# Loading the border rows and the first tile of a pooling mixer in single loads, with another order of its loads and steps

## The chip, the cores and the metric

The program runs on one core of a Trainium2 chip. The metric is the device time of one execution in microseconds; the lower, the better. A core has engines that run side by side, each through its own list of instructions in order: TensorE (PE) does matrix products, VectorE (DVE), ScalarE (ACT) and GpSimd (POOL) work on tiles, SyncE (SP) issues loads and stores. They wait for each other through semaphores.

## The reference, cut to what matters

A trunk of two layers on 512 tokens of width 1024, in float32. Layer 0 mixes tokens by pooling, layer 1 by stick-breaking attention; each mixer is followed by an MLP with a squared ReLU, and every block is wrapped in RMS norms. The change lies in the pooling mixer of layer 0, which is the first thing that the program does:

```
def pool_mixer(h, w_grp, scale):            # h: (1, 512, 1024)
    cp = cumsum of h along the tokens, with a zero in front
    for g, w in enumerate((2, 4, 8, 16)):   # four groups of 256 channels
        window sum over the last w tokens / min(pos + 1, w) - h
    y = einsum('bsgc,gcd->bsgd', y, w_grp)  # 256 x 256 per group
    return y * scale

x = x + rms_norm(pool_mixer(rms_norm(x, mix_pre_g[0]), pool_w[0], pool_scale[0]), mix_post_g[0])
h = rms_norm(x, mlp_pre_g[0])
x = x + rms_norm(square(relu(h @ w_up[0])) @ w_down[0], mlp_post_g[0])
...                                          # layer 1: attention, then its MLP
```

## The kernel before, in words

The 512 tokens lie in four tiles x0 to x3 of 128 tokens each, with the channels along the free axis. Pooling is a matrix product: for each group of channels a banded matrix of 128 x 128 (`bands`) holds the window's weights less the identity. The band is scaled row by row with the token's reciprocal norm and multiplied on TensorE with the tile. The first 15 tokens of tiles 1 to 3 need rows of the tile before, so the 30 rows around each of the three borders are held apart in a fourth operand, `edge` (90 rows), which has a band of its own with 46 columns.

The mixer is written as steps, each a letter with a tile (0 to 3; 4 is `edge`) and mostly a half h of the channels. The list `MIX_ORDER` names the steps one after another, and every engine runs its own steps in that order; nothing else sorts them. The letters that matter here:

- `z n`: n products of a constant bf16 tile into a bank that nobody reads (`busy`, function at L652 to L654): it only keeps TensorE at work.
- `S h`, `C h`: the channel scale, one row in memory, is spread over 128 partitions by a product with ones (PE, L658) and copied to `scale` (ACT, L661).
- `L i b`: a 256-column piece of the group weights `pw` is multiplied by the norm's gain (`gc`) and by `scale` (DVE, L667).
- `q t`, `r t`, `b t`: sum of squares of a tile (ACT, L679), its power -0.5 (POOL, L690), the scaled band (DVE, L698).
- `P t h`, `c t h`: the pooling product (PE, L708) and its copy to `yt` (ACT, L723; three pieces for `edge`, L719).
- `M t h`, `s t h`, `g t h`: the group product of `yt` with `pw` (PE, L731), its sum of squares (ACT, through L250), its product with the gain row (DVE, L739).
- `e`, `E`, `A`: norm and residual; `w`, `v`, `N`: the next norm; `T`, `H`, `X`: transposes (PE, L765) and the split of the result into a high and a low float32r part (ACT L773, DVE L777).
- `h j`, `l j`, `U j`: the same split for the first four blocks of the MLP's up weights (ACT L785, DVE L789) and their product with the first 256 tokens (PE, L607 to L609). `U0` is the first product of the MLP.

All loads before are issued by SP, in the order in which they are written. A load's tile is not waited for by SP itself; but the program has eight semaphores for loads in turn, so that SP issues a load only after the load eight places earlier has landed.

From `U0` on the program is a long stream of products: the MLP of layer 0 (its down product in Strassen-Winograd form, L497), the projections and attention, the second MLP. The table that the change replaces ends with `U0` to `U3`.

Of the kernel before, what the change touches and what calls it, by code (L numbers as in the profile page):

```python
# [15 lines left out]
P = 128  # L16
D = 1024
S = 512
# [13 lines left out]
TS = [slice(t * P, (t + 1) * P) for t in range(T)]  # L32
NS = [slice(0, 512), slice(512, 1024)]
# [7 lines left out]

MIX_ORDER = [
    (w[0], [int(c) for c in w[1:]])
    for w in """z8 q0 S0 r0 C0 b0 S1 z1 P00 L01 C1 L02 L00 P01 L03 L12 c00 c01 M00 q4 L10 r4 L11 s00 L13 b4 q1 r1 M01 s01
    e0 P40 b1 P11 P10 q2 c40 r2 c11 E0 q3 g00 b2 g01 r3 c10 P21 A0 b3 M11 w0 M10 s11 c21 v0 P31 N00 g11 s10
    T00 P30 h0 M21 e1 c31 g10 E1 c30 N01 A1 P20 H00 T01 w1 X00 h1 v1 l0 s21 N11 M30 T11 c20 N10 T10 H01 M20
    l1 H11 X11 H10 X10 s30 M31 X01 h2 s20 h3 g21 l2 s31 g20 e2 g30 E2 e3 E3 U0 A2 w2 g31 U1 A3 v2 U2 l3 N20
    w3 T20 H20 v3 N31 T31 N30 N21 T30 H31 X20 X31 T21 H30 X30 U3 H21 X21""".split()
]


# [10 lines left out]
EDGE, REST, BORDER = 30, 114, 46  # L62
# [7 lines left out]
def trunk(ctx, tc, x, consts, gcol, grow, pw, wup, wdn, wq, wk, wv, wo, out):  # L70
    nc = tc.nc
# [4 lines left out]
    psum = pool("psum", 8, space=bass.MemoryType.PSUM)  # L76
    dram = pool("dram", space=bass.MemoryType.DRAM)

    nc.scalar.preload_act_table_set("sigmoid_and_others")

    uid = [0]

    def name(s):
# [7 lines left out]
    xt = [keep.tile([P, D + 2], F32, tag=f"x{t}", name=f"x{t}") for t in range(T)]  # L91
    ident = keep.tile([P, P], F32, tag="ident", name="ident")
    gc = keep.tile([P, 3 * KC + 32], F32, tag="gc", name="gc")[:, : 3 * KC]
    for n in NS:
        nc.sync.dma_start(xt[0][:, n], x[TS[0], n])
    mhalf = keep.tile([P, 1], F32, tag="mhalf", name="mhalf")
    nc.vector.memset(mhalf, -0.5)

# [123 lines left out]
    for l in range(2):  # L222
        if l == 1:
            n = len(queue)
# [387 lines left out]
    with tc.tile_pool(name="mix0", bufs=1, reuse_waits="tile") as mp:  # L612
# [7 lines left out]
        edge = mp.tile([3 * EDGE, D + 2], F32, tag="edge", name="edge")  # L620
# [4 lines left out]
        BANDS = (P, REST, BORDER)  # L625
        starts = [0, 4 * P, 4 * (P + REST)]
        bands = mp.tile([P, 4 * sum(BANDS)], F32, tag="bands", name="bands")
        wpool = [mp.tile([P, D], F32, tag=f"pw{i}", name=f"pw{i}") for i in range(2)]
        nc.sync.dma_start(bands[:, : 4 * P], consts[:, P : 5 * P])
        nc.sync.dma_start(row[:1], grow[R_SCALE : R_SCALE + 1, :])  # L630
        nc.sync.dma_start(gc, gcol)
        for i in range(2):
            nc.sync.dma_start(wpool[i], pw[i])
        for i in range(3):
            lo = (i + 1) * P - EDGE // 2
            nc.sync.dma_start(edge[i * EDGE : (i + 1) * EDGE, :D], x[lo : lo + EDGE, :])
        nc.sync.dma_start(xt[1][:, :D], x[TS[1], :])
        nc.sync.dma_start(bands[:, 4 * P :], consts[:, 5 * P :])
        nc.sync.dma_start(xt[2][:, :D], x[TS[2], :])
        gpost = gain_row(R_MIX_POST0)  # L640
        nc.sync.dma_start(xt[3][:, :D], x[TS[3], :])
# [171 lines left out]
    with tc.tile_pool(name="att", bufs=1, reuse_waits="tile") as ap:  # L813
# [79 lines left out]
        for lo, n in SEG.values():  # L893
            c = min(n - P, 1)
            d = begin[:, lo + n - P - c : lo + n]
# [178 lines left out]
```

## Time and profile before

| | |
|---|---|
| time, median of 3 runs | 963.49 us (961.94 to 963.75) |
| profiled execution: its time, its span | 967.47 us, 965.7 us |
| busy share of the span: PE, PEld, DVE, ACT, POOL | 98%, 83%, 74%, 59%, 15% |
| mean granted TensorE clock | 0.991 |
| instructions | 12404 |
| moved by the DMA engines | 157.03 MB, 163 GB/s on average |

The span runs from the first instruction to the last; the 1.77 us between it and the execution's own time lie around it. PE is TensorE's products, PEld its loads of the stationary operand, which overlap them. The granted clock is the share of TensorE's full rate that the chip let it have. In a table of stretches each row gives, for one stretch of time, the busy microseconds of every engine with the number of instructions in brackets, then the granted clock, the mean busy share of the 16 DMA engines and what they moved in GB/s.

### The profile page before, as it was taken

What the parts mean: (1) busy time and instruction counts of PE and PEld (TensorE: products, weight loads), DVE (VectorE), ACT (ScalarE), POOL (GpSimd) and SP (SyncE); (2) the same over time, 40 slices, a digit from 0 to 9 for tenths busy, and PEclk for the clock granted to TensorE, in tenths of its full rate; (3) what the DMA queues carried; (4) which work ended last, traced back from release to release, by engine and by line L of the source; (5) the groups of instructions that cost most, each with busy time, mean ns of one, the idle gap of its engine ahead of it and who ended that gap; (6) DMA issues with size and microseconds to landing.
All of it is one profiled execution on the core that took longest, in us unless ns stands there. A gap on an engine that the chain in (4) does not pass through costs nothing.

```text
span 965.7 us, 12404 instructions
## 1 busy us (share of the span) xinstructions
PE 947.1 (98%) x4761; PEld 806.2 (83%) x4761; DVE 711.1 (74%) x736; ACT 566.9 (59%) x974; POOL 142.1 (15%) x108
## 2 busy tenths in 40 slices
PE   8999999999999999999999999989999999999997
PEld 6998888888788888899799997888888888888885
DVE  3865798997988966576477787855596776957956
ACT  5667889697684747456666562546445454443632
POOL 1210310402203114000000000302040300303003
PEclk8999999999999999999999999999999999999999
DMA  7343979688596850521534233231513233132012
GB/s 261 135 173 123 354 234 356 259 283 327 199 354 249 311 194 1 200 98 53 219 130 174 88 139 124 108 133 66 190 50 131 109 106 135 44 131 109 27 40 87
DMA packets 43683, 157.03 MB, mean 163 GB/s; under 512 B 4494, under 2 KB 4878, under 8 KB 43625
## 3 DMA queue, kind: packets, MB, share of 16 engines
q1 hardware_dynamic: 43625, 156.25, 45.4%
q8 instruction: 37, 0.61, 0.2%
q14 instruction: 21, 0.17, 0.1%
HBM read 122.68 MB, written 33.55 MB: 162 GB/s over the span
## 4 chain that ended last, share of the span: by engine, by line
PE 73%; DVE 11%; DMA 5%; issue 5%; ACT 5%; POOL 0%; POOLq 0%; DVEq 0%; SPq 0%; ACTq 0%
PE ps L497 18%; PE ps L608 11%; PE ps L607 11%; PE ps L609 11%; PE ps L268 4%; PE ps L269 4%; PE ps L267 4%; DMA xn<-in_wdn 3%; DVE w L247 2%; DMA raw<-in_wup 2%; PE ps L957 2%; PE ps L947 2%; DVE w L134 2%; DVE e L471 2%; PE ps L731 1%
## 5 line engine op out<-in xcount | busy, mean ns | idle before, releaser
L497 PE MATMUL ps<-w,a 128*128 128x512 f32 x1176 | 278.2, 390 | 1.2 <-DVE a L247 1.2
L608 PE MATMUL ps<-xnl,w 128*128 128x512 f32 (+1 forms) x712 | 262.8, 369 | 0.1
L609 PE MATMUL ps<-xnh,w 128*128 128x512 f32 (+1 forms) x712 | 262.5, 369 | 0.0
L607 PE MATMUL ps<-xnh,w 128*128 128x512 f32 (+1 forms) x712 | 262.4, 370 | 0.0
L497 PEld LDWEIGHTS ps<-w,a 128*128 128x128 f32 x1176 | 220.6, 188 | 48.0 <-DVE a L247 2.4
L609 PEld LDWEIGHTS ps<-xnh,w 128*128 128x128 f32 x712 | 135.0, 190 | 22.2
L608 PEld LDWEIGHTS ps<-xnl,w 128*128 128x128 f32 x712 | 135.0, 190 | 22.0 <-DVE xnl L247 0.3
L607 PEld LDWEIGHTS ps<-xnh,w 128*128 128x128 f32 x712 | 134.7, 190 | 21.8
L134 DVE TENSOR_TENSOR w<-raw,w 128x1024 fp32r<-128x1024 f32 x62 | 82.3, 1327 | 65.3 <-ACT w L132 65.2
L132 ACT CAST w<-raw 128x1024 fp32r<-128x1024 f32 x62 | 64.9, 1049 | 81.4 <-PE ps L609 76.2
L506 DVE TENSOR_TENSOR y<-ps,y 128x512 f32<-128x512 f32 x124 | 83.1, 683 | 33.2 <-PE ps L497 33.1
L246 ACT CAST a<-r 128x768 fp32r<-128x768 f32 (+1 forms) x60 | 47.6, 793 | 63.3 <-PE ps L497 39.2
L452 POOL TENSOR_TENSOR s<-r 128x768 f32<-128x768 f32 (+1 forms) x10 | 21.4, 2144 | 371.3 <-ACT r L530 352.7
L246 ACT CAST w<-e 128x1536 fp32r<-128x1536 f32 (+1 forms) x30 | 42.0, 1399 | 53.8 <-DVE e L471 42.6
L247 DVE TENSOR_TENSOR a<-r,a 128x768 fp32r<-128x768 f32 (+1 forms) x60 | 60.0, 1002 | 16.5 <-ACT a L246 16.4
L292 POOL TENSOR_TENSOR y<-y,grow 128x512 f32<-128x512 f32 x12 | 18.7, 1562 | 314.2 <-ACT xn L250 314.2
L247 DVE TENSOR_TENSOR w<-e,w 128x1536 fp32r<-128x1536 f32 (+1 forms) x30 | 59.6, 1988 | 3.1 <-ACT w L246 2.7
L452 POOL TENSOR_TENSOR r<-r 128x768 f32<-128x768 f32 (+1 forms) x20 | 50.5, 2523 | 66.1 <-DVE a L247 65.3
L929 DVE TENSOR_TENSOR_SCAN e<-u,begin 128x1280 f32<-128x1280 f32 x16 | 45.1, 2822 | 13.3 <-ACT u L923 13.0
L143 ACT ACTIVATE apart<-apart,gc 128x128 f32<-128x128 f32 (+1 forms) x132 | 43.0, 407 | 0.0
L250 ACT ACTIVATE xn<-y 128x512 f32<-128x512 f32 (+1 forms) x25 | 15.4, 616 | 41.6 <-DVE y L359 41.5
L529 ACT ACTIVATE r<-ps 128x512 f32<-128x512 f32 x56 | 33.0, 590 | 6.8 <-PE ps L609 6.8
(137 smaller groups left out, 1492.5 us busy)
## 6 DMA issues: line engine op xcount, KB each, us to landing
raw<-in_wup SPq DMA_DIRECT2D x62, 512.0 KB, 3.9
w<-kept SPq DMA_DIRECT2D x58, 512.0 KB, 4.2
kept<-wx SPq DMA_DIRECT2D x30, 512.0 KB, 5.0
w<-in_wdn SPq DMA_DIRECT2D x8, 1536.0 KB, 6.7
kept<-apart SPq DMA_DIRECT2D x24, 512.0 KB, 4.3
xn<-in_wdn SPq DMA_DIRECT2D x8, 1536.0 KB, 9.2
raw<-in_wdn SPq DMA_DIRECT2D x8, 512.0 KB, 3.7
apart<-in_wk SPq DMA_DIRECT2D x7, 512.0 KB, 6.4
```

The lines of the kernel that those rows point to most:

```text
L132: nc.scalar.copy(hi, raw)
L134: nc.vector.tensor_tensor(out=lo, in0=raw, in1=hi.bitcast(F32), op=ALU.subtract)
L143: nc.scalar.mul(c, c, gc[:, lo + k : lo + k + 1])
L246: latest["act"] = nc.scalar.copy(hi, src)
L247: latest["dve"] = nc.vector.tensor_tensor(out=lo, in0=src, in1=hi.bitcast(F32), op=ALU.subtract)
L452: sub = lambda out, x, y, op=ALU.subtract: nc.gpsimd.tensor_tensor(out=out, in0=x, in1=y, op=op)
L497: nc.tensor.matmul(bank, a[:, x, q, TS[t]], w[:, z, q], start=start and q == 0 and k == 0, stop=q == self.n - 1 and k == 2, skip_group_che ...
L506: nc.vector.tensor_tensor(out=part, in0=bank, in1=part, op=ALU.add)
L607: nc.tensor.matmul(pu[:, cols], wh[:, k, :], xnh[:, k, cols], start=k == 0, stop=False)
L608: nc.tensor.matmul(pu[:, cols], wh[:, k, :], xnl[:, k, cols], start=False, stop=False)
L609: nc.tensor.matmul(pu[:, cols], wl[:, k, :], xnh[:, k, cols], start=False, stop=k == KC - 1)
L929: nc.vector.tensor_tensor_scan(out=e[:, ::-1], data0=u[:, 1:][:, ::-1], data1=begin[:, ::-1], initial=0.0, op0=ALU.mult, op1=ALU.max,)
```

## The change

1. The first tile x0 comes in one load of 128 x 1024 instead of two of 128 x 512.
2. The norm columns `gc` are issued by ACT's queue, ahead of its table load, instead of by SP.
3. The three loads of border rows become one: a view of x with three dimensions (3 borders, 30 rows, 1024 channels) is written to the 90 rows of `edge`.
4. The order of the loads: `pw0` now stands ahead of the scale row, and the second part of `bands` ahead of x1.
5. `MIX_ORDER` is another list. It holds the same steps and two `z2` more, that is four more constant products.

```diff
 MIX_ORDER = [
     ...
-    for w in """z8 q0 S0 r0 C0 b0 S1 z1 P00 L01 C1 L02 L00 P01 L03 L12 c00 c01 M00 q4 L10 r4 L11 s00 L13 b4 q1 r1 M01 s01
-    e0 P40 b1 P11 P10 q2 c40 r2 c11 E0 q3 g00 b2 g01 r3 c10 P21 A0 b3 M11 w0 M10 s11 c21 v0 P31 N00 g11 s10
+    for w in """z8 S0 q0 r0 C0 S1 C1 b0 L03 z1 P00 c00 L00 P01 c01 q4 L02 L01 r4 L13 L11 L10 M00 L12 b4 s00 q1 M01 s01 r1
+    q2 b1 e0 r2 g01 z2 P40 c40 z2 P10 P11 c10 M10 c11 M11 g00 E0 q3 A0 w0 r3 b2 v0 b3 s10 N00 g10 P20 P30 s11 P31
...
-    nc.scalar.preload_act_table_set("sigmoid_and_others")
...
-    for n in NS:
-        nc.sync.dma_start(xt[0][:, n], x[TS[0], n])
+    nc.sync.dma_start(xt[0][:, :D], x[TS[0], :])
+    nc.scalar.dma_start(gc, gcol)
+    nc.scalar.preload_act_table_set("sigmoid_and_others")
...
-        nc.sync.dma_start(bands[:, : 4 * P], consts[:, P : 5 * P])
+        nc.sync.dma_start(wpool[0], pw[0])
         nc.sync.dma_start(row[:1], grow[R_SCALE : R_SCALE + 1, :])
-        nc.sync.dma_start(gc, gcol)
-        for i in range(2):
-            nc.sync.dma_start(wpool[i], pw[i])
-        for i in range(3):
-            lo = (i + 1) * P - EDGE // 2
-            nc.sync.dma_start(edge[i * EDGE : (i + 1) * EDGE, :D], x[lo : lo + EDGE, :])
+        nc.sync.dma_start(wpool[1], pw[1])
+        around = x[P - EDGE // 2 : S - EDGE // 2, :].rearrange("(i r) d -> i r d", r=P)[:, :EDGE]
+        nc.sync.dma_start(edge[:, :D], around)
+        nc.sync.dma_start(bands[:, 4 * P :], consts[:, 5 * P :])
         nc.sync.dma_start(xt[1][:, :D], x[TS[1], :])
-        nc.sync.dma_start(bands[:, 4 * P :], consts[:, 5 * P :])
         nc.sync.dma_start(xt[2][:, :D], x[TS[2], :])
```

(The load of the first part of `bands` is still issued, right behind x0.)

Two places show how the order moves. The first is SP's list of loads from the program's start. Before (`x_70` is x0, `x_71` x1, `x_72` x2; `pw_99` and `pw_100` are the two halves of the group weights):

```order
L95 DMA x_70<-in_x 128x512 x2
L629 DMA bands<-in_consts 128x512
L630 DMA row<-in_grow 1x1024
L631 DMA gc<-in_gcol 128x24
L633 DMA pw_99<-in_pw 128x1024
L633 DMA pw_100<-in_pw 128x1024
L636 DMA edge<-in_x 30x1024 x3
L637 DMA x_71<-in_x 128x1024
L638 DMA bands<-in_consts 128x640
L639 DMA x_72<-in_x 128x1024
```

Before, the scale row was the fourth load and stood ahead of 1 MB of `pw`.

After (`x_69`, `x_70`, `x_71` are x0, x1, x2; `pw_100` and `pw_101` the two halves):

```order
L92 DMA x_69<-in_x 128x1024
L627 DMA bands<-in_consts 128x512
L629 DMA pw_100<-in_pw 128x1024
L630 DMA row<-in_grow 1x1024
L631 DMA pw_101<-in_pw 128x1024
L633 DMA edge<-in_x 90x1x1024
L634 DMA bands<-in_consts 128x640
L635 DMA x_70<-in_x 128x1024
L636 DMA x_71<-in_x 128x1024
```

The scale row moved behind the first half of `pw`, `edge` became one load, and x1 moved behind the rest of `bands`.

The second place is TensorE between the pooling of tile 0 and that of tile 2, around the product with `edge`. Before:

```order
L708 MATMUL ps_152<-band_138,x_70 128x128 x4
L731 MATMUL ps_161<-pw_99,yt 128x256 x4
L731 MATMUL ps_178<-pw_100,yt 128x256 x4
L708 MATMUL ps_185<-band_173,edge 128x46 x8
L708 MATMUL ps_196<-band_194,x_71 128x114 x4
L708 MATMUL ps_201<-band_194,x_71 128x114 x4
L708 MATMUL ps_223<-band_218,x_72 128x114 x4
L731 MATMUL ps_231<-pw_100,yt 128x256 x4
L731 MATMUL ps_237<-pw_99,yt 128x256 x4
```

Here the product with `edge` is followed by three pooling products (two of x1, one of x2) and then by the two group products of tile 1.

After, from the two group products of tile 0 on:

```order
L728 MATMUL ps_163<-pw_100,yt 128x256 x4
L728 MATMUL ps_174<-pw_101,yt 128x256 x4
L651 LDWEIGHTS warm
L651 MATMUL ps_118<-warm 128x512
L651 LDWEIGHTS warm
L651 MATMUL ps_118<-warm 128x512
L705 MATMUL ps_191<-band_169,edge 128x46 x8
L651 LDWEIGHTS warm
L651 MATMUL ps_118<-warm 128x512
L651 LDWEIGHTS warm
L651 MATMUL ps_118<-warm 128x512
L705 MATMUL ps_205<-band_183,x_70 128x114 x4
```

Two constant products now stand ahead of the product with `edge` and two behind it. Behind these rows come the second pooling product of x1 and the group products of tile 1, and only then those of x2 and x3. From `U0` on every engine's list is the same as before.

More of the change, by code (lines that the diff above doesn't have):

```diff
@@ L43 @@
     (w[0], [int(c) for c in w[1:]])
-    for w in """z8 q0 S0 r0 C0 b0 S1 z1 P00 L01 C1 L02 L00 P01 L03 L12 c00 c01 M00 q4 L10 r4 L11 s00 L13 b4 q1 r1 M01 s01
-    e0 P40 b1 P11 P10 q2 c40 r2 c11 E0 q3 g00 b2 g01 r3 c10 P21 A0 b3 M11 w0 M10 s11 c21 v0 P31 N00 g11 s10
-    T00 P30 h0 M21 e1 c31 g10 E1 c30 N01 A1 P20 H00 T01 w1 X00 h1 v1 l0 s21 N11 M30 T11 c20 N10 T10 H01 M20
-    l1 H11 X11 H10 X10 s30 M31 X01 h2 s20 h3 g21 l2 s31 g20 e2 g30 E2 e3 E3 U0 A2 w2 g31 U1 A3 v2 U2 l3 N20
-    w3 T20 H20 v3 N31 T31 N30 N21 T30 H31 X20 X31 T21 H30 X30 U3 H21 X21""".split()
+    for w in """z8 S0 q0 r0 C0 S1 C1 b0 L03 z1 P00 c00 L00 P01 c01 q4 L02 L01 r4 L13 L11 L10 M00 L12 b4 s00 q1 M01 s01 r1
+    q2 b1 e0 r2 g01 z2 P40 c40 z2 P10 P11 c10 M10 c11 M11 g00 E0 q3 A0 w0 r3 b2 v0 b3 s10 N00 g10 P20 P30 s11 P31
+    h0 e1 E1 c20 g11 A1 N01 c30 c31 P21 T00 H00 w1 h1 l0 M20 v1 X00 c21 s20 M30 T01 N11 T11 s30 N10 T10 H11
+    l1 H10 g30 X11 H01 M21 M31 s21 h2 s31 X10 X01 g21 U0 g20 e2 E2 l2 e3 U1 g31 A2 E3 h3 w2 v2 A3 l3 U2 N21
+    w3 v3 N20 T20 N30 T30 H20 H30 N31 X20 T21 T31 H31 X30 U3 H21 X31 X21""".split()
 ]
@@ L627, in trunk @@
         bands = mp.tile([P, 4 * sum(BANDS)], F32, tag="bands", name="bands")
+        nc.sync.dma_start(bands[:, : 4 * P], consts[:, P : 5 * P])
         wpool = [mp.tile([P, D], F32, tag=f"pw{i}", name=f"pw{i}") for i in range(2)]
-        nc.sync.dma_start(bands[:, : 4 * P], consts[:, P : 5 * P])
+        nc.sync.dma_start(wpool[0], pw[0])
         nc.sync.dma_start(row[:1], grow[R_SCALE : R_SCALE + 1, :])
-        nc.sync.dma_start(gc, gcol)
-        for i in range(2):
-            nc.sync.dma_start(wpool[i], pw[i])
-        for i in range(3):
-            lo = (i + 1) * P - EDGE // 2
-            nc.sync.dma_start(edge[i * EDGE : (i + 1) * EDGE, :D], x[lo : lo + EDGE, :])
+        nc.sync.dma_start(wpool[1], pw[1])
+        around = x[P - EDGE // 2 : S - EDGE // 2, :].rearrange("(i r) d -> i r d", r=P)[:, :EDGE]
+        nc.sync.dma_start(edge[:, :D], around)
+        nc.sync.dma_start(bands[:, 4 * P :], consts[:, 5 * P :])
         nc.sync.dma_start(xt[1][:, :D], x[TS[1], :])
-        nc.sync.dma_start(bands[:, 4 * P :], consts[:, 5 * P :])
         nc.sync.dma_start(xt[2][:, :D], x[TS[2], :])
```

## The prediction

> **What bounds the kernel now.** I read the table of stretches first, then TensorE's instructions in order of time, then the waits behind the mixer. TensorE up to `U0`:
>
> ```profile
> 1.31 3.59 PE L654 MATMUL ps<-warm 128*128 128x512 bf16 x8 [1.31 <-POOL warm L615]
> 4.82 3.08 PE L658 MATMUL ps<-row,ones 128*128 128x512 f32 x4
> 7.73 0.38 PE L654 MATMUL ps<-warm 128*128 128x512 bf16 x1
> 7.95 1.95 PE L708 MATMUL ps<-band,x 128*128 128x128 f32 x16
> 10.80 3.84 PE L731 MATMUL ps<-pw,yt 128*128 128x256 f32 x16 [0.90 <-ACT yt L723]
> 15.44 1.98 PE L708 MATMUL ps<-band,edge 90*128 90x46 f32 x16 [0.80 <-DVE band L698]
> 17.70 5.47 PE L708 MATMUL ps<-band,x 128*128 128x114 f32 x24 [0.28 <-DVE band L698]
> 22.95 4.23 PE L731 MATMUL ps<-pw,yt 128*128 128x256 f32 x16
> ...
> 34.87 3.62 PE L731 MATMUL ps<-pw,yt 128*128 128x256 f32 x16
> 38.14 0.47 PE L607 MATMUL ps<-xnh,w 128*128 128x256 f32 x1
> ```
>
> Columns are start and length; the bracket is idle time before the row and what ended it. TensorE waits 0.90, 0.80 and 0.28 us in the mixer, and from 17.70 to `U0` at 38.1 it never waits. Behind that:
>
> ```profile
> PE ps L324 <- DVE xn L315: 3.3, 1, 3.3
> PE ps L268 <- DVE w L134: 2.2, 2, 2.0
> PE ps L497 <- DVE a L247: 1.2, 3, 0.6
> PE ps L267 <- DVE al L247: 0.7, 1, 0.7
> PE ps L267 <- DVE kl L871: 0.5, 1, 0.5
> PE ps L267 <- ACT xnh L246: 0.2, 1, 0.2
> ```
>
> From 38.2 us to the end TensorE waits 8.1 us in all (us, times, longest). So what moves `U0` moves nearly the whole program, and the change is worth what it moves `U0`. Now the clock (busy time per engine, then the granted clock, the DMA share and GB/s):
>
> ```profile
> 13.91:17.32 3.41, 2.61 (x20) 2.16 (x18) 0.57 (x3) 3.28 (x9) 1.10 (x2) 1.00 1.03 414
> 17.32:20.74 3.42, 3.14 (x15) 3.04 (x15) 2.70 (x5) 2.31 (x7) 1.08 (x2) 0.50 0.87 353
> 20.74:24.15 3.41, 3.41 (x15) 3.23 (x15) 1.43 (x3) 2.21 (x5) 1.09 (x2) 0.50 0.06 20
> 24.15:27.56 3.41, 3.41 (x19) 3.04 (x19) 1.03 (x2) 1.40 (x4) 0.00 (x0) 1.00 0.00 0
> 464.47:467.88 3.41, 2.48 (x10) 1.42 (x9) 3.35 (x6) 3.36 (x8) 0.00 (x0) 1.00 1.03 419
> 580.52:583.94 3.42, 1.45 (x8) 1.09 (x7) 3.26 (x5) 0.00 (x0) 0.00 (x0) 1.00 0.13 12
> 628.31:631.72 3.41, 2.25 (x20) 2.01 (x18) 2.27 (x4) 2.08 (x5) 0.45 (x1) 1.00 0.80 302
> 631.72:635.14 3.42, 1.27 (x10) 1.09 (x11) 2.00 (x5) 0.81 (x3) 0.55 (x1) 1.00 0.02 6
> 17.70:38.12 20.42, 20.42 (x112) 19.02 (x113) 14.46 (x21) 15.14 (x34) 3.54 (x6) 0.84 0.28 104
> ```
>
> The first busy time in each row is that of TensorE's products. From 17.32 to 24.15 us the clock stands at 0.50: 6.83 us at half speed, 3.41 us lost, in the stretch where TensorE is the bound (mean 0.84 there). DVE and ACT are busy 14.46 and 15.14 of 20.42 us, so a TensorE that is faster by 3.4 us is still the slowest of them (17.0).
>
> What brought the drop: the stretch ahead of it looks busy (2.61), but most of it is the product with `edge`, whose matmuls stream 46 columns in the time in which others stream 114. The chain of waits gives the lengths at full clock:
>
> ```profile
> 4.91 2.99 PE ps L658 x4
> 7.90 0.22 PE ps L654
> 8.11 1.80 PE ps L708 x16
> 27.18 0.88 PE ps L708 x8
> 35.04 3.46 PE ps L731 x16
> ```
>
> A pooling matmul takes 0.88/8 = 0.11 us. The 16 on `edge` take about 1.9 us (15.44 to 17.36), and by columns I count them as 46/114 of that, 0.77. With 0.7 us of group products before 14.64 the stretch holds about 1.5 us of streaming. Stretches with 1.45 and 1.27 also dropped; those with 2.48 and 2.25 did not. So I place the limit between 1.5 and 2.25 us out of 3.41.
>
> [...]
>
> **The change, part by part.** The loads and what waits for them:
>
> ```profile
> 4.00:6.00 2.00, 2.00 (x5) 0.70 (x3) 0.00 (x0) 1.15 (x2) 0.05 (x1) 1.00 0.97 314
> 4.72 1.06 ACT L679 ACTIVATE junk<-x 128x1025 f32<-128x1025 f32 x1 [2.71 <-DMA x<-in_x]
> 13.26 1.06 ACT L679 ACTIVATE junk<-edge 90x1025 f32<-90x1025 f32 x1 [2.74 <-DMA edge<-in_x]
> 15.16 1.06 ACT L679 ACTIVATE junk<-x 128x1025 f32<-128x1025 f32 x1
> 17.19 0.45 DVE L698 TENSOR_SCALAR band<-bands,stat 128x456 f32<-128x456 f32 x1
> 2.51 0.35 SPq L631 DMA_DIRECT2D gc<-in_gcol x1
> 3.84 1.56 SPq L636 DMA_DIRECT2D edge<-in_x x3
> 5.45 0.71 SPq L637 DMA_DIRECT2D x<-in_x  x1
> ```
>
> *x0 in one load, `gc` by ACT.* SP saves about 0.43 us of issue (1.56/3 is 0.52, 0.35 for `gc`) on each; ACT spends as much ahead of its table load, hidden under the 2.71 us in which it waits for x0. x0 may land 0 to 0.4 us earlier. Nothing is gained, since the next term is later.
>
> *The scale row behind `pw0`.* `S0` needs it and stands second on TensorE. Before, it came just in time: `S0` followed the eighth warm-up product at 4.9. Now 512 KB of `pw0` are queued ahead: 0.51 MB at 314 GB/s is 1.7 us. Bounds 0 (if the row overtakes) and +1.7; the issues saved ahead of it take some 0.5 off. I take `S0` at 6.0, +1.1 us. Queued behind `S0` on TensorE is everything, `P00` included.
>
> *Does that reach `P10`?* From 6.0: 2.99 for the scale, 0.22, 1.80 for `P00` and `P01`, 3.46 for `M00` and `M01` end at 14.5. Before, they ended at 14.64, with the wait of 0.90 and some 0.4 of waiting inside `M`, which are now covered because `pw0` is early and the copies run ahead. But a pause before `S0` costs clock: the first eight products take 0.45 us each, the one at 7.9 takes 0.22, so the clock rose at about 7 after some 5.7 us of work (though the table gives 1.00 from the start). With 1.1 us of pause in it the half rate lasts perhaps 3.4 us longer, and the products in that stretch cost up to 1.4 us more. So `M01` ends between 14.5 and 15.9.
>
> *`edge` in one load.* Three issues become one, so SP is free for x1 about 1 us sooner. That matters little where the DMA engines are busy at 1.03 of their share. Spread over all of them, 360 KB at 414 GB/s take 0.9 us, and the load would land near 10. But the new source has an outermost dimension of 3. If it takes only three of 16 engines, 414/16 = 26 GB/s each, then 360 KB need 4.7 us behind `pw1`. With x0 in at about 4.7 and 1.3 MB (`bands`, both `pw`) behind it at 314 to 414 GB/s, `pw1` is in between 7.9 and 8.9; at 8.2 `edge` lands at 12.9, and everything queued behind it on these three lands after it. Between 10 and 12.9 I take 12.9, beside which the 13.26 of before lies nearest: `P40` can start at 15.1 (2.18 us after ACT's start, as before).
>
> [...] No row before shows such a load. [...]
>
> *x1 behind the rest of `bands`.* 320 KB (0.8 us) and x1's own 512 KB (1.3 us) after 12.9: 15.0. Before, `b1` ended 2.48 us after ACT took up x1 at 15.16; now about 17.5. No change at this term (-0.2 to +0.8).
>
> *Two `z2`.* Four products of 0.22 us at full clock (0.43 at half), two on either side of `P40`: `P40` from the later of 15.1 and `M01` + 0.43 (14.9 to 16.3), 1.9 us, then 0.43 more. `P10` starts at 17.6 to 18.7. I take 18.2, +0.5 us against 17.70.
>
> *What they do to the clock.* A stretch of 3.41 us that holds all of `P40` now has 0.77 + 0.86 and 0.7 us of dense products around: 2.3, above the 2.25 that kept the clock, if nothing waits beside it; a wait of 0.7 us would undo it. From `P10` to `U0` the 20.42 us shrink to 17.0 without the low clock, 18.7 with one such stretch. Bounds -3.4 and 0; I take -2.6, three quarters, since both places where TensorE may pause (before `S0`, before `P40`) still depend on loads.
>
> *The reordered middle* (x1's products ahead of x2's and x3's, `M`, `T` and DVE's steps in another order): the same work, no instruction more. It can cost 0 to 0.5 us where a copy is late (`c40` and `c10` now stand behind the squares of x2), and I take 0.2. *Later:* three waits for DVE in the first MLP (1.2 us) and those near 464 us swallow part of an earlier start; 0 to 0.9, I take 0.4.
>
> **Sum**, against the profiled execution: +0.5 - 2.6 + 0.2 + 0.4 = -1.5 us, so 967.47 becomes 966.0. The median of the three runs is 4.0 us below the profiled execution, and its clock isn't shown; I carry the difference over: 963.49 - 1.5 = 962.0. About 0.2%, 1.93 us, can be told from no change here, and the runs shown spread over 1.8 us.
>
> **Rivals.**
> 1. The clock holds and the loads are no later: `P10` at 17.6 (-0.1), the full -3.4, 0 to 0.4 given back: -3.2, 960.3. For it: the kept stretch with 2.25; against it: `S0`'s pause.
> 2. Slower: the row's pause keeps TensorE at half rate until `P40`. Then `P10` comes at 18.7 or, if the row needs its whole 1.7 us, at 19.3, and one to two low stretches remain. At +1.6 with the loss unchanged, 0.2 in the middle and nothing given back: +1.8, about 965.3. It decides when the pause before `S0` passes some 1.5 us. For it: `pw0`'s 512 KB; against it: the pause is made up by waits of 2.0 us that were there before.
> 3. The edge load confined to three engines delays more than I count: 90 rows through three engines at the slower rate of 4 to 6 us (314/16 = 20 GB/s) take 6.1 us, it lands at 14.3, and x1 at 16.4; `P40` at 16.5, `P10` at 19.0, but the clock kept as in the sum: +1.3 - 2.6 + 0.6 = -0.7, 962.8. [...]
> 4. The change does nothing for the clock and nothing is late: 963.5.
>
> **Chances.** My forecast 0.44 (of it 0.15 beyond 1.93 us); rival 1 0.23; rival 2 0.12; rival 3 0.12 and rival 4 0.09, all within 0.2%. So faster 0.15 + 0.23 = 0.38, same 0.29 + 0.21 = 0.50, slower 0.12. The range reaches to rival 1 with a little more (959.6) and to rival 2 (965.3), and leaves out about 0.1 on each side.
>
> **What the new profile would show.** `S0` at 5.5 to 6.6 with idle time before it, ended by the row's load; `edge`'s squares on ACT at 12.5 to 14; DMA share well below 1 in some stretch around 9 to 13 if three engines carry `edge`; `P10` near 18.2; the clock at 1.00 from 17 to 24, or one low stretch instead of two; `U0` near 36.2 instead of 38.1; the waits after it as before. I am wrong if the row lands before 4.9 (then rival 1), if the clock stays low through the early products into 17 (rival 2), or if DVE or ACT becomes the wait before `U0`.

## The result, and the profile after

The changed kernel takes 969.31 us (median of 15 runs, 966.12 to 969.86). The kernel before, run beside it, takes 962.85 us (15 runs, 961.19 to 967.15). The ratio is 1.0056 with an interval of 1.0044 to 1.0068, which is about 5.4 us slower by the ratio and 6.5 us between the medians. I had forecast 962.0 us, with 959.6 to 965.3 as the range. The profiled execution took 969.65 us, 2.18 us more than the profiled one of before; that one (967.47 us) was slower than any of those 15 runs of the kernel before, so the two profiles show less than half of the loss.

TensorE up to `U0`, in order of time (start, length, idle time before the row and what ended it):

```profile
1.31 3.59 PE L651 MATMUL ps<-warm 128*128 128x512 bf16 x8 [1.31 <-POOL warm L614]
6.57 1.96 PE L655 MATMUL ps<-row,ones 128*128 128x512 f32 x4 [1.67 <-DMA row<-in_grow]
8.37 0.38 PE L651 MATMUL ps<-warm 128*128 128x512 bf16 x1
8.58 1.95 PE L705 MATMUL ps<-band,x 128*128 128x128 f32 x16
10.37 3.67 PE L728 MATMUL ps<-pw,yt 128*128 128x256 f32 x16
13.87 0.59 PE L651 MATMUL ps<-warm 128*128 128x512 bf16 x2
18.23 3.26 PE L705 MATMUL ps<-band,edge 90*128 90x46 f32 x16 [3.77 <-DVE band L695]
21.71 0.63 PE L651 MATMUL ps<-warm 128*128 128x512 bf16 x1 [0.22 <-issue]
22.14 3.55 PE L705 MATMUL ps<-band,x 128*128 128x114 f32 x16
...
37.76 3.62 PE L728 MATMUL ps<-pw,yt 128*128 128x256 f32 x16
41.02 0.47 PE L606 MATMUL ps<-xnh,w 128*128 128x256 f32 x1
```

`U0` comes at 41.02 us and not at 38.14. TensorE stands idle for 3.77 us ahead of `P40`, and `P40` itself takes 3.26 us where it took 1.98. It also waits 1.67 us for the scale row ahead of `S0`. The rest of the program waits as before, except for two waits at 251 and 256 us, in the down product of the first MLP (line 496):

```profile
PE ps L705 <- DVE band L695: 3.8, 1, 3.8
PE ps L323 <- DVE xn L314: 3.3, 1, 3.3
PE ps L267 <- DVE w L133: 2.2, 2, 2.0
PE ps L655 <- DMA row<-in_grow: 1.7, 1, 1.7
PE ps L496 <- DVE a L246: 1.4, 1, 1.4
PE ps L496 <- DVE w L246: 1.3, 1, 1.3
```

The band that `P40` waits for is the end of a short chain. ACT's squares of `edge` start when the border load has landed:

```profile
16.05 1.06 ACT L676 ACTIVATE junk<-edge 90x1025 f32<-90x1025 f32 x1 [4.90 <-DMA edge<-in_x]
```

SP's next load, of MLP weights, is issued behind the same landing:

```profile
15.97 0.91 SPq L779 DMA_DIRECT2D raw<-in_wup  x2
```

The chain of work that ended last shows the load as one piece (start, length):

```profile
2.89 13.06 DMA edge<-in_x
```

Issued at 2.89, it landed at 2.89 + 13.06 = 15.95 us. Last, the stretches (clock, DMA share and GB/s are the last three numbers of a row):

```profile
8.00:10.00 2.00, 2.00 (x16) 1.64 (x15) 1.67 (x5) 1.21 (x3) 0.00 (x0) 1.00 1.05 334
10.00:12.00 2.00, 2.00 (x13) 1.82 (x13) 1.58 (x4) 0.84 (x2) 0.00 (x0) 1.00 1.04 217
12.00:14.00 2.00, 2.00 (x11) 1.64 (x10) 0.00 (x0) 0.00 (x0) 0.00 (x0) 1.00 1.05 227
...
18.00:20.00 2.00, 1.77 (x10) 1.77 (x11) 0.41 (x2) 1.94 (x5) 0.55 (x1) 0.67 1.02 403
15.27:18.69 3.42, 0.46 (x4) 0.46 (x5) 0.31 (x1) 2.57 (x5) 0.55 (x1) 1.00 1.02 378
18.69:22.10 3.41, 3.19 (x15) 3.08 (x16) 1.87 (x4) 2.83 (x9) 1.57 (x3) 0.50 0.58 232
22.10:25.51 3.41, 3.41 (x17) 3.37 (x16) 1.65 (x2) 0.55 (x2) 0.05 (x1) 0.50 0.14 59
22.14:41.02 18.88, 18.88 (x113) 17.62 (x112) 13.06 (x19) 13.82 (x29) 2.21 (x5) 0.91 0.21 67
```

Two things are to be seen. While the border load is under way the DMA engines' share stays at 1.04 to 1.05, yet they move 217 to 227 GB/s, half of the 403 of later: the engines count as busy, and their packets are slow (in the trace's records 4 KB packets take 311 ns at the median from 10 to 14 us and 159 ns from 16 to 20 us). And the stretch in which TensorE had only 0.46 us of work (15.27 to 18.69) is followed by two at half clock. The two that the change was to remove are there again, later.

### The profile page after: what moved, and what is told of

It is laid out like the page before. It is cut to its first block, busy times and chain, and to the rows that moved or that the text cites. A ratio compares the mean times of both kernels' runs of the same rounds, so it can differ in the third digit from the quotient of the medians.

```text
span 967.8 us, 12406 instructions
## 1 busy us (share of the span) xinstructions
PE 944.3 (98%) x4764; PEld 804.5 (83%) x4765; DVE 710.6 (73%) x736; ACT 567.7 (59%) x974; POOL 145.2 (15%) x108
## 4 chain that ended last, share of the span: by engine, by line
PE 78%; DVE 9%; DMA 5%; issue 4%; ACT 3%; POOL 0%; SPq 0%; POOLq 0%; DVEq 0%; ACTq 0%
PE ps L496 21%; PE ps L606 12%; PE ps L607 12%; PE ps L608 12%; PE ps L267 4%; PE ps L268 4%; PE ps L266 4%; DMA xn<-in_wdn 2%; PE ps L954 2%; DVE w L246 2%; PE ps L944 1%; DMA edge<-in_x 1%; DVE w L133 1%; DVE e L470 1%; DMA apart<-in_wq 1%
## 5 line engine op out<-in xcount | busy, mean ns | idle before, releaser
L505 DVE TENSOR_TENSOR y<-ps,y 128x512 f32<-128x512 f32 x124 | 83.2, 683 | 34.6 <-PE ps L496 34.5
L451 POOL TENSOR_TENSOR r<-r 128x768 f32<-128x768 f32 (+1 forms) x20 | 53.2, 2662 | 66.2 <-DVE a L246 65.4
L246 DVE TENSOR_TENSOR w<-xn,w 128x1536 fp32r<-128x1536 f32 (+1 forms) x20 | 33.0, 1651 | 5.5 <-ACT w L245 5.5
```

What stands on the lines that cost most here:

```text
L246: latest["dve"] = nc.vector.tensor_tensor(out=lo, in0=src, in1=hi.bitcast(F32), op=ALU.subtract)
L451: sub = lambda out, x, y, op=ALU.subtract: nc.gpsimd.tensor_tensor(out=out, in0=x, in1=y, op=op)
L505: nc.vector.tensor_tensor(out=part, in0=bank, in1=part, op=ALU.add)
```

## The experiments

The main theory: three engines alone carry the border load, whose source has an outermost dimension of 3 (my supposition, which no row of before shows), and its late landing is the whole loss. The rivals: a single load is slow as such; the scale row's new place or the new list costs the time. The expectation in front of each result calls `U0` the first up block. Unless said otherwise each experiment is an edit of the changed kernel.

**Three border loads in place of one, the rest of the change kept.**

```diff
-        around = x[P - EDGE // 2 : S - EDGE // 2, :].rearrange("(i r) d -> i r d", r=P)[:, :EDGE]
-        nc.sync.dma_start(edge[:, :D], around)
+        for i in range(3):
+            lo = (i + 1) * P - EDGE // 2
+            nc.sync.dma_start(edge[i * EDGE : (i + 1) * EDGE, :D], x[lo : lo + EDGE, :])
```

> The changed kernel with the border rows again in three loads of 30 rows; all else as changed. Theory A (the single load runs on three engines and lands at 16.0 instead of about 13): the squares of the border rows start near 13, the product with edge near 15.5 to 16 instead of 18.2, U0 at 37.5 to 38.5 instead of 41.0, and the time falls from 969.3 to 962 to 965. Theory B (the late scale row and the new list of steps cost the time, the border load only fills a gap that is there anyway): 967.5 to 969.5. Theory C (half a share each): about 966.

964.33 us, ratio 1.0006 (0.9994 to 1.0018). Its profile (TensorE, in order of time):

```profile
6.57 2.91 PE L656 MATMUL ps<-row,ones 128*128 128x512 f32 x4 [2.04 <-DMA row<-in_grow]
...
9.71 2.49 PE L706 MATMUL ps<-band,x 128*128 128x128 f32 x16
...
15.97 1.88 PE L706 MATMUL ps<-band,edge 90*128 90x46 f32 x16
...
35.39 0.47 PE L606 MATMUL ps<-xnh,w 128*128 128x256 f32 x1
```

The loss is gone, and so is the wait ahead of `P40`. `U0` comes 2 us earlier than Theory A said, and the time is within its range. What is left of the change gains nothing that these runs can tell.

**The kernel before, with the border rows in one load.** The edit is the reverse of the one above, in the kernel before.

> The kernel before with the border rows in one load; all else as before. Theory A: the load lands near 16 or later, the product with edge starts near 18, and the time rises by 4 to 6 us to 967 to 969. Theory B: within 1 us of before, 962 to 964.

970.76 us, ratio 1.0073 (1.0054 to 1.0091): this one part of the change alone makes the whole loss, and a little more than Theory A said. The squares on ACT wait for the load as in the changed kernel:

```profile
17.09 1.06 ACT L678 ACTIVATE junk<-edge 90x1025 f32<-90x1025 f32 x1 [7.48 <-DMA edge<-in_x]
```

and TensorE for the squares:

```profile
19.26 3.65 PE L707 MATMUL ps<-band,edge 90*128 90x46 f32 x16 [6.66 <-DVE band L697]
...
42.58 0.47 PE L607 MATMUL ps<-xnh,w 128*128 128x256 f32 x1
```

**One load, but its rows interleaved, so that the outermost dimension is 30.** Partition 3r + i now holds row r of border i; the constant `border` bands are permuted alike.

```diff
-        around = ....rearrange("(i r) d -> i r d", r=P)[:, :EDGE]
+        around = ....rearrange("(i r) d -> r i d", r=P)[:EDGE]
...
-            at[i * EDGE : (i + 1) * EDGE, i * cut : (i + 1) * cut] = later[:EDGE, cut:EDGE]
+            at[i : 3 * EDGE : 3, i * cut : (i + 1) * cut] = later[:EDGE, cut:EDGE]
```

> The changed kernel, the border rows still in one load, but laid out row by row over the three borders (partition 3r+i instead of 30i+r, the constant border bands permuted to match), so that the source's outermost dimension is 30 instead of 3. [...] Rival A2 (a single load of many rows is slow as such, because its rows crowd a few partitions or because the loads behind it are at work beside it): lands at 15 to 16, 967 to 969.5.

962.2 us, ratio 0.9992 (0.9982 to 1.0001). `P40` no longer waits:

```profile
14.29 1.88 PE L705 MATMUL ps<-band,edge 90*128 90x46 f32 x16
...
16.44 1.94 PE L705 MATMUL ps<-band,x 128*128 128x114 f32 x16
...
33.71 0.47 PE L606 MATMUL ps<-xnh,w 128*128 128x256 f32 x1
```

One load of the same 90 rows costs nothing, so a single load is not slow as such; what differs is the order of its rows. It landed by 10.27 us, far ahead of the 15 to 16 of Rival A2, since SP's next load waits for that landing; in the changed kernel that next load is issued at 15.97 us.

The expectations further down call this the load on fifteen engines, and the kernel with it the fifteen-engine version. The number is an estimate of mine from the traces' records of landings. For the border load with three pieces the trace of the changed kernel has one early record (4.19 us) and three late ones (14.97, 15.63 and 15.95), which I count as three engines. For the first of the three loads of 30 rows the trace of before has one early (4.45) and fifteen late ones (8.12 to 12.25), so I count fifteen for a load with 30 rows outermost. For the interleaved load itself no run shows the number.

**The scale row ahead of the first pool weights**, in the changed kernel:

```diff
-        nc.sync.dma_start(wpool[0], pw[0])
         nc.sync.dma_start(row[:1], grow[R_SCALE : R_SCALE + 1, :])
+        nc.sync.dma_start(wpool[0], pw[0])
```

> The changed kernel with the scale row ahead of the first half of pw, as before; border rows in one load. Theory A: S0 starts at 4.9 instead of 6.6, but the product with edge still waits for its load until 18 and so does everything behind it: 968.5 to 969.8. Theory B: the 1.7 us come back: 967 to 968.

971.28 us, ratio 1.008 (1.0065 to 1.0094; 4 runs). `S0` comes at 5.22, 1.35 us earlier, and nothing of it is left at `P40`:

```profile
5.22 2.80 PE L655 MATMUL ps<-row,ones 128*128 128x512 f32 x4 [0.31 <-DMA row<-in_grow]
...
19.97 3.65 PE L705 MATMUL ps<-band,edge 90*128 90x46 f32 x16 [6.02 <-DVE band L695]
```

Its border load landed still later (squares at 17.79). So the scale row's place is hidden behind the late border rows. Why the load took 1.7 us longer here isn't settled.

**The same swap with the interleaved load.**

> The border load on fifteen engines, and the scale row's load ahead of the first pool weights. In the fifteen-engine version the scale row lands at 6.43 us and TensorE waits 1.7 us for it, and nothing waits later before the first up block (34.6 us). Theory R (TensorE's order is then the limit, so an earlier scale row is an earlier everything): S0 at 5.2 us, first up block at about 33.4, time about 1.0 to 1.5 us under that version, 960.7 to 961.2. Rival Q (something else than the scale row, such as the pool weights or the border rows' bands, ends the waits behind S0): first up block within 0.4 us of 34.6, time 962.2 as that version, ratio to the kernel before 0.999.

961.06 us, ratio 0.9971 (0.9959 to 0.9984): faster than the kernel before and, by 8.3 us in the medians, than the changed one. The earlier scale row now seems to count: 0.44 us at `U0`, 1.1 us between the medians of the two interleaved versions, 2.0 us by their ratios, whose intervals touch. The 34.6 us that the expectation gives for the first up block of the interleaved version isn't that version's `U0`, which stands at 33.71; the shift is therefore 0.44 us and not the 1.2 of Theory R, though the time fell as it said. So `U0` hardly tells the theory from its rival.

```profile
5.24 2.84 PE L655 MATMUL ps<-row,ones 128*128 128x512 f32 x4 [0.34 <-DMA row<-in_grow]
...
33.27 0.47 PE L606 MATMUL ps<-xnh,w 128*128 128x256 f32 x1
```

**The old list.** Two versions keep the changed kernel's loads, with the interleaved border load, and put the old `MIX_ORDER` back: one with the scale row second to `pw0`, one with it first.

> The changed kernel's loads with the border rows on fifteen engines, but the old list of the mixer's steps. It differs from the fifteen-engine version by the list alone. Theory L1 (the new list suits these loads and gives most of what is left of the gain): 1.5 to 3 us slower than that version, 963.7 to 965.2, with waits of TensorE of that size ahead of the first up block. Rival L2 (the list is worth under 0.5 us once the border rows land early): 961.7 to 962.7.

962.06 us, ratio 0.9984 (0.9971 to 0.9997), against 962.2 with the new list.

> The changed kernel's loads with the border rows on fifteen engines and the scale row ahead of the first pool weights, and the old list of the mixer's steps. It differs from the row-first version (961.06 us, ratio 0.9971) by the list alone. Theory L2, which stands since the two lists timed alike behind the later scale row (962.06 and 962.20): again alike, 960.5 to 961.6, first up block at 32 to 33.5 us. Rival L3 (the new list is worth something once the scale row is early): 961.8 to 963.5, with a wait of TensorE for scaled bands ahead of the first up block.

962.07 us, ratio 0.9996 (0.9981 to 1.001), against 961.06 with the new list. `U0` stands at 32.97 and 33.15 us, 0.74 and 0.12 us ahead of where it stands with the new list (33.71 and 33.27), so the new list gains nothing up to there. The 1.0 us between the last two medians fits the rival's range, and TensorE waits 0.32 us for the border's scaled bands ahead of `P40`, as the rival said; but the two intervals touch and `U0` is no later, so whether the list is worth something there stays open.

**The kernel before, with its three border loads replaced by the interleaved one.**

> The kernel before, with its three border loads replaced by one on fifteen engines; its order of loads and its list stay. Theory G (the landing of the border rows, 13.1 us, is what holds the kernel before, which waits 1.1 us for the border's scaled bands and then runs at half clock from 16.4 to 24): they land near 10.5, the wait goes, and so does the half clock; 960 to 961. Rival H (TensorE waits for something else in its place, since the old list has other work ahead of it): 962.7 to 963.7, ratio 1.000.

962.5 us, ratio 0.999 (0.9975 to 1.0005). `P40` starts at 13.63 and not at 15.44, but it still waits for its band, and so does the product behind it:

```profile
13.63 1.98 PE L707 MATMUL ps<-band,edge 90*128 90x46 f32 x16 [0.50 <-DVE band L697]
15.83 4.56 PE L707 MATMUL ps<-band,x 128*128 128x114 f32 x24 [0.22 <-DVE band L697]
```

One stretch of half clock stays (16.7 to 20.1). So Theory G was wrong that the waits and the half clock would go. The interval holds no change; neither 960 nor a plain nothing is shown.

**Without the two `z2`**, in the row-first version with the interleaved load:

```diff
-    q2 b1 e0 r2 g01 z2 P40 c40 z2 P10 P11 ...
+    q2 b1 e0 r2 g01 P40 c40 P10 P11 ...
```

> The row-first version on fifteen engines without the two pairs of constant products (z2) that the new list puts ahead of P40 and of P10. Theory Z1 (with the border rows early these products hide no wait, and TensorE's order is the limit): each pair is 0.43 us of TensorE's time, P40 starts at 13.4 in place of 13.85 and P10 at 15.1 to 15.3 in place of 16.0; first up block 0.5 to 0.9 earlier, 32.4 to 32.8; time 960.2 to 960.6. Rival Z2 (the pairs keep the clock up: without them a stretch of half clock comes between 13 and 24 us): first up block 34 or later, 961.5 to 963.

960.35 us, ratio 0.9974 (0.9962 to 0.9986), the same as with them within the intervals. No half clock shows in the mixer without them, in this one profile: the 16 pooling products of x1 take 2.04 us (3.55 us at half clock in the changed kernel), and the mean clock of the execution is 0.996. `P40` at 13.66 waits 0.24 us for its band. `U0` comes at 33.09 and not at 33.27, so 0.2 us of the 0.9 that the products take come back, less than the 0.5 that Theory Z1 gave as its least: without them TensorE waits in part of their time. They aren't needed for the clock here and cost well under a microsecond.

**Why the packets were slow.** The border rows from another tensor, in the same three pieces:

```diff
-        around = x[P - EDGE // 2 : S - EDGE // 2, :].rearrange("(i r) d -> i r d", r=P)[:, :EDGE]
+        around = pw.rearrange("a p d -> (a p) d")[: 3 * 80].rearrange("(i r) d -> i r d", r=80)[:, :EDGE]
```

> The changed kernel, whose one border load (90 rows of 4 KB in three pieces) reads 90 rows of the pool weights and no rows of x: the border tokens' results are then wrong, the work is the same. It asks why the load took to 15.97 us and not to the 12.9 that 26 GB/s for each of three engines gives, and why the rate of all loads fell to 217 to 227 GB/s while it was under way. Theory X (rows of x that are read twice at about the same time, by the border load and by the loads of x, come slowly): it lands at 12.5 to 13.5, GB/s between 10 and 14 us stay above 300, time 963 to 966. Rival Y (the form of the load itself slows all, whatever it reads): lands near 16, 217 to 230 GB/s, 968.5 to 970.

968.31 us, ratio 1.0044 (1.0029 to 1.006), squares of `edge` at 16.05, and the same low rate. Rows of x that are read twice are not the cause. The pool weights are loaded just ahead of the border load, so these rows too are read twice; that reading rows twice does no harm as such is shown only further down, by the block of tokens 128 to 255, which x1's load reads again.

```profile
10.00:12.00 2.00, 2.00 (x19) 1.97 (x18) 2.00 (x7) 1.17 (x3) 0.00 (x0) 1.00 1.05 221
12.00:14.00 2.00, 2.00 (x11) 1.77 (x10) 0.45 (x2) 0.51 (x1) 0.00 (x0) 1.00 1.05 229
```

The load with three pieces moved behind all other early loads:

> The changed kernel with its border load (three pieces, on three engines) moved behind the gain row of the first MLP, the last of the early loads: it then runs with nearly nothing beside it. It asks why its packets took twice the time of others. Theory S (three engines alone go at full rate, 26 GB/s each, and they are slow only beside others): while it runs alone the windows show about 78 GB/s, it takes 4.6 to 5 us from the end of the other loads. Rival T (its own packets are slow, whatever runs beside them): about 40 GB/s, 9 us. Either way the border's squares start at 20 us or later, so P40 and all behind it are late: 972 to 980.

976.18 us in one run, beside 962.63. Its stretches:

```profile
8.00:10.00 2.00, 2.00 (x17) 1.69 (x15) 1.76 (x5) 1.21 (x3) 0.00 (x0) 1.00 1.02 417
...
16.00:18.00 2.00, 0.00 (x0) 0.00 (x0) 0.00 (x0) 0.00 (x0) 0.00 (x0) 1.00 0.97 287
...
20.00:22.00 2.00, 0.00 (x0) 0.00 (x0) 0.00 (x0) 0.28 (x1) 0.00 (x0) 0.50 0.19 80
```

Without the border load, 8 to 10 us move 417 GB/s. With it beside loads of MLP weights it is 287. From 20 us on, when the other loads are done, it is 80 GB/s at a DMA share of 0.19 of 16 engines, as much as 3.0 engines that are busy all the time; the border's squares start at 21.72. With the three late landings above I take it that the load runs on three. That makes 26.7 GB/s for each, as much as each of sixteen has at 417 (26), an estimate. So, as far as this one run shows, the load is slow only beside others, and it slows the others too (287 against 417 GB/s).

Three other forms in the place of the border load: 128 rows in sixteen pieces of eight rows, 96 KB apart; one block of 128 rows; and 90 rows (tokens 128 to 217) that follow one on another (`edges` is the same tile with 128 rows; only the new lines are shown, and the comments number them):

```diff
+        around = x[: 3 * P, :].rearrange("(a r) d -> a r d", r=24)[:, :8]    # first
+        nc.sync.dma_start(edges[:, :D], x[P : 2 * P, :])                     # second
+        nc.sync.dma_start(edge[:, :D], x[P : P + 3 * EDGE, :])               # third
```

> The changed kernel, whose border load brings 128 rows in sixteen pieces of eight rows (of tokens 0 to 383, so the border tokens' results are wrong) in place of 90 rows in three pieces; the computation uses 90 of them as before. [...] It asks whether the fall of the rate (288 GB/s between 8 and 10 us in the fifteen-engine version, 217 to 227 in the changed kernel) goes with the split of rows over engines. [...] Rival W (a load of rows that do not follow one on another slows them whatever its split): below 320 GB/s while it is under way, landing at 9.8 or later. [...]

```profile
8.00:10.00 2.00, 2.00 (x14) 1.50 (x13) 1.46 (x4) 1.21 (x3) 0.00 (x0) 1.00 1.01 234
```

> The changed kernel, whose border load brings tokens 128 to 255 as one block of 128 rows that follow one on another, exactly as a token tile's load, into the border's place (the border tokens' results are then wrong). With the sixteen pieces of eight rows that lie 96 KB apart the rate fell to 234 GB/s between 8 and 10 us. Theory W (pieces of the source that lie apart slow all the loads): with one block the rate stays above 380 GB/s from 6 to 12 us, the border's squares start by 10.5 us. Rival D (what slows them is the place that is written, or the place in the queue): again below 300 GB/s between 8 and 10 us, and a landing after 10.2.

```profile
8.00:10.00 2.00, 2.00 (x6) 1.10 (x5) 1.61 (x5) 0.94 (x2) 0.00 (x0) 0.50 1.05 422
```

> [...] Theory W: as with one block, no fall of the rate. [...]

```profile
8.00:10.00 2.00, 2.00 (x6) 0.92 (x5) 1.58 (x4) 0.97 (x2) 0.00 (x0) 0.50 1.01 332
```

Single runs of 962.01, 962.26 and 964.37 us (the kernel before: 962.63, 964.73, 964.73). In the first the border's squares start at 11.26 us; in the other two SP's next load behind the landing is issued at 9.29 and 9.40 us. The same stretch with three plain loads of 30 rows (first row) and with the interleaved load (second row):

```profile
8.00:10.00 2.00, 2.00 (x5) 0.77 (x4) 1.57 (x4) 0.88 (x2) 0.00 (x0) 0.50 0.99 225
8.00:10.00 2.00, 2.00 (x16) 1.64 (x15) 1.68 (x5) 1.21 (x3) 0.00 (x0) 1.00 1.02 288
```

The block is as fast as any load (422 GB/s), so neither the place written nor the place in the queue slows them, nor that its rows are read twice. (Its squares start at 12.77 and not by 10.5, because the copies of `P00` and `P01` stand ahead of them on ACT and came late; the load had landed by 9.29.) Pieces that lie apart do slow them, in pieces of eight rows too (234). Only this one distance of 96 KB was tried with eight rows, so it isn't shown whether the distance itself matters. 90 rows in a row fell between (332, where Theory W had no fall), and the three plain loads of 30 rows, each in a row, gave 225. So the pieces are one cause and not the only one; what the other is, and how either works inside the chip, isn't shown.

## Why the prediction was wrong, point by point

- **"`edge` in one load" is the step that failed, by its size.** Three engines were in the sum, at 26 GB/s each beside others: 4.7 us from 8.2, landing at 12.9. No row of before shows a load on three engines, so the term was a guess; the runs showed the three late landings and, with the load alone, 80 GB/s (20 to 22 us above), which fit three engines at 26 GB/s. Beside other loads that rate didn't hold, and the packets of all engines were slow: in the trace's records of them, 4 KB packets take 159 ns at the median from 16 to 20 us and 311 ns from 10 to 14 us. Measured is a landing at 15.95, which is 7.75 us from 8.2 and not 4.7: for thirty packets in a row on each of three engines 258 ns each (an estimate, with the 8.2 of the prediction). Rival 3 was nearer for the load, with 20 GB/s for each engine and a landing at 14.3; the measured one is beyond it too, and the clock that it kept was lost. The row to read was in the kernel before: its stretch from 8 to 10 us, in which by their order its own border loads ran, shows this:

```profile
8.00:10.00 2.00, 1.90 (x17) 1.71 (x15) 0.58 (x2) 1.17 (x3) 0.00 (x0) 1.00 0.99 229
10.00:12.00 2.00, 1.20 (x6) 1.10 (x7) 1.40 (x4) 0.52 (x1) 0.00 (x0) 1.00 0.99 274
```

  At 229/16 = 14 GB/s for each engine, 360 KB on three take 8.4 us, and from 8.2 the load lands at 16.6, by this estimate. I took the rates of 4 to 6 us and of 14 to 17 us, on either side of the border loads.
- **The sign I named was wrong.** Three engines were to show as a DMA share well below 1 between 9 and 13 us. It read 1.04 to 1.05, with slow packets on the others too (311 ns, as above); the fall was in GB/s (217 to 227).
- **The clock, -2.6, followed from that term and fell with it.** I had written that a wait of 0.7 us beside `P40` would undo it; the wait was 3.77 us. The four `z2` products, which I had counted for the clock, weren't needed for it: in the version without them the mixer shows no half clock either. (The row of `P40` before ends at 17.42 and not at 17.36; nothing hangs on it.) Two half-rate stretches came (18.69 to 25.51), and the first holds `P40`, which so took 1.3 us longer. In the interleaved version, where no wait comes ahead of `P40`, the clock reads 1.00 in every row up to 520 us. The low stretches start at 18.69 us here (6.82 us long), at 7.42 in the first experiment (3.41 us long) and at 17.79 in the second; what sets their starts isn't shown. Nor is a limit as such: the 1.5 to 2.25 us of work that I gave was an estimate from five stretches of before, and here 0.46 us stands ahead of the low stretch and 2.60 us (11.86 to 15.27 us) ahead of none.
- **`P10` at 18.2** came at 22.14: 3.9 us late, of which P40's late start is 1.9 to 3.1 (18.23 against 15.1 to 16.3) and P40's slow clock 1.3.
- **The scale row, +1.1** (6.0): it came at 6.57, the upper bound, with the idle time of 1.67 us ended by the row's load as I had said. Behind it TensorE caught up: `M01` ended at 14.04, even ahead of the 14.5 I gave. Half clock in the early products, rival 2 on a small scale, came in other versions with the same late row: from 7.42 to 10.83 in the first experiment (`P00` and `P01` 2.49 us), from 7.9 to 11.3 with the block and from 7.8 to 11.2 with the 90 rows in a row. In the first experiment it is the whole 1.68 us by which `U0` there (35.39) is behind that of the interleaved version (33.71).
- **x0, `gc`, the middle**: as said. (Not every engine's list is the same from `U0` on, as I had written: the two lists differ in order up to `U3`. TensorE waits for nothing there in either profile.) From `P10` to `U0` it took 18.88 us with 3.37 us at half clock, so 17.2 at full clock; the interleaved version took 17.27. Forecast were 17.0 and 0.2 for the middle.
- **"Later", +0.4**: the waits in the first MLP's down product are 2.7 us and were 1.2, so +1.5; I had them swallow part of an earlier start, and nothing started earlier. Why they grew isn't shown. Those near 464 us are 1.4 us in both. The stretch of half clock near 584 us isn't there in this profile (1.7 us less). Of the eight profiles with a row from 576 to 591 us, those of both kernels among them, four read a clock of 0.89 there, which is one such stretch, and four 1.00.
- **The base.** The profiled execution of before has a mean clock of 0.991, and 23 runs of that kernel beside the first experiments show 0.993 to 0.996, 0.995 in the middle. In the interleaved version a mean clock of 0.995 goes with two stretches of half clock of 3.41 us, not counting the one at the very end, and in the profile of before 0.991 goes with four; one of them lies between 626 and 642 us in all eight profiles with a row there (0.89). By that count a typical run of the kernel before has at most one such stretch in the mixer, so at most 1.7 of the 3.4 us that I offered to gain were there (an estimate: no trace of a typical run was kept). Carried over to the median, the -2.6 was thus too large even with an early border load. The interleaved version, with no half clock left in the mixer, is only 1.0 us under the median of before, and its interval holds no change. That its 962.2 us lie next to my 962.0 is luck and doesn't bear out the sum: between the profiles its `U0` is 4.4 us earlier, and I had forecast 1.9.

Profile against profile the parts are: `U0` 2.88 later (`P10` 4.44 later, the stretch behind it 1.56 shorter), 1.5 more in the first MLP, 1.7 less near 584. That is 2.7 us, against 2.2 measured; the other 0.5 isn't accounted for.

## What to carry to other kernels

Merging loads saves issues on a queue (SP took 0.88 us for the one border load and 1.56 for the three), and here the issues were worth nothing that the runs can tell; what counted was the form of the merged load: with 3 x 30 rows it landed at 15.95 us and with 30 x 3 by 10.27, so put the longest dimension outermost, even if a constant has to be permuted for it, and look at the landing. Price a load by the GB/s of the stretch in which the same rows were loaded before, not by the best stretch, and look at GB/s beside the DMA share, since slow packets count as busy (217 GB/s at a share of 1.04). When a gain rests on the clock, look first whether the profiled execution is a typical one: its mean clock beside that of the other runs tells.

## What the runs showed of the hardware

While a border load ran whose source lies in three pieces of 30 rows or in sixteen of eight, the DMA engines moved 217 to 234 GB/s in all in the rows shown above, from either of two tensors; without it they moved 417 and with one block of 128 rows in its place 422. With the rows interleaved it was 288, and 287 where the three pieces came behind all other early loads. Pieces that lie apart aren't the only case: three loads of 30 rows, each in a row, gave 225. The busy share of the DMA engines stayed at 0.97 to 1.05 in all these rows.
